# A hybrid retention, delta-net and RG-LRU block in fp32: mixer outputs, the delta net's values and keys and the retention's keys turned by VectorE in 32x32 blocks and stored with 128-byte runs

## The chip, the cores and the metric

The kernel runs on one core of a Trainium2 chip. The metric is the device time of one execution in microseconds, given as the median over several runs. One more execution was recorded by the hardware profiler; all views of the profile are from that one.

## The reference

Two layers work on one sequence of 1024 tokens with 1024 channels, all in float32. What matters here is the mixer of the first layer:

```
q_r,k_r,v_r,g_r, q_d,k_d,v_d,g_d, b_d,a_d = split(hn @ w_in)       # hn = rms_norm(h)
q_r, k_r = rotary(q_r), rotary(k_r)                                # 4 heads of 128
y_r = rms(retention_chunkwise(q_r, k_r, v_r)) * silu(g_r)          # chunks of 128
q_d,k_d,v_d = silu(causal_conv(...)); q_d,k_d = l2norm(q_d), l2norm(k_d)
y_d = rms_norm(gated_delta_chunkwise(q_d, k_d, v_d, g, beta), gain) * silu(g_d)
h = h + concat(y_r, y_d) @ w_out
```

In the delta net every chunk computes u = T (beta v - ... k S), out = (q S) + (masked q k^T) u, and S = S * decay + k_tail^T u, where T is the inverse of a triangular matrix. The retention has the same shape without the triangular solve. Before the mixers stands an RMS norm, behind each layer a convolutional feed-forward network; the second layer's mixer is a gated linear recurrence.

## The kernel before, in words

Activations lie with channels on the 128 partitions and tokens along the free axis. A float32 matrix is split into a high and a low part, and each product is three matmuls, lines 313, 314 and 315 (one "slot" in the code). A weight quarter of 128x512 is loaded by SyncE's queue (line 257), cast by ScalarE to its high part (line 267) and subtracted by VectorE (line 268); the rings hold six split quarters and seven raw ones. A projection of 128 output channels is 48 such matmuls: two halves of 512 tokens, 8 slots each. Each half has a PSUM bank of the tag "pp", of which there are four, and so has each output tile of the mixers.

The first mixer (`_mix0`) projects one unit of 128 channels after another. The order around the change is: the delta net's keys (kept in K), its queries, two gates, its values (`conv_head("v", h)`, convolution at lines 1263 to 1268), one more gate, and then, per head, the retention's query and key (`rot_head`: the rotary product is lines 1537, 1539 and 1540 on VectorE and line 1541 on GpSimd). The triangular inverses of the delta net are made from 32x32 blocks by `merge` (lines 1368 to 1399), one per head, with steps on TensorE and ScalarE in turn. They run beside the projections: a lane takes one step every two slots.

After the values, two lanes run beside the retention's projections:

- `scans` takes the delta net's eight chunks in order. `scan_inside` prepares a chunk: the decay mask (lines 1452, 1454), the values scaled by beta (line 1461), the scores k q (lines 1464, 1465), the scaled key tail (line 1473). `scan_state` does the chain: k S (line 1484), v minus it (line 1486), T v (line 1490, copied by ScalarE in line 1492 to u), k_tail^T u (line 1497), the new state (line 1502), and the output (lines 1507, 1508).
- `ret_half` takes one head and 512 tokens: scores (1576), key tail (1586), kv (1591), the states (1597, 1599), output (1605, 1606). It has one buffer for the values (`rvt`) and one for the key tail (`rkt`).

An output tile goes through `normalise`: square on ScalarE (1414), row sums and scaling on VectorE, a power on GpSimd (1421), the product (1423), and eight slots later `post`.

Five places turn 128x128 tiles by a TensorE matmul against the identity: `post` (line 1428, tokens to channels, copied out of PSUM by ScalarE in line 1429 and stored by ScalarE's queue), the delta net's values (line 1460) and keys (line 1472), and the retention's keys (line 1584).

The program's order on each engine is not the order of the code: a scheduler places the instructions by priority and by its own estimate of when they are ready, except in stretches marked as manual. Each engine then runs its list strictly in order, each instruction waiting for semaphores. At most eight DMAs of the SyncE and ScalarE queues use eight semaphores in turn.

Of the kernel before, what the change touches and what calls it, by code (L numbers as in the profile page):

```python
# [13 lines left out]
F32 = mybir.dt.float32  # L14
# [5 lines left out]
P = 128  # L20
# [3 lines left out]
HALF = 512  # L24
# [79 lines left out]
class Block:  # L104
# [1039 lines left out]
    def mix0(self, gain):  # L1144
        tc = self.tc
        self.q_dram = tc.dram_tile([NCH, P, HALF], F32, name="q_dram")
        self.v_dram = tc.dram_tile([NCH, P, HALF], F32, name="v_dram")
        self.gc_dram = tc.dram_tile([NH, NCH, P], F32, name="gc_dram")
        self.l_dram = tc.dram_tile([P, 32, 32], F32, name="l_dram")
        self.t_dram = tc.dram_tile([2, P, 32, 32], F32, name="t_dram")  # L1150
        self.y_dram = tc.dram_tile([8, P, T], F32, name="y_dram")
        self.rv_dram = tc.dram_tile([NCH, P, HALF], F32, name="rv_dram")
        self.g_dram = tc.dram_tile([NH, P, T], F32, name="g_dram")
        self.X = [[(self.slots1(4 * k + n), self.slots1(4 * k + 2 + n)) for n in range(2)] for k in range(KT)]
        with tc.tile_pool(name="l0", bufs=1) as pool:
            gd = self._mix0(pool.tile([P, 24 * HALF], F32, name="l0"))
        self.s2_stack = ExitStack()
        self.open_s2(self.s2_stack)
        self._mix0_out(gain, gd)
# [10 lines left out]
    def _mix0(self, room):  # L1170
# [239 lines left out]
        def normalise(o, eps, ydst, i):  # L1410
# [13 lines left out]

            def post():
                p = self.pc()
                for h in range(4):
                    PE.transpose(p[:, hs(h)], on[:, hs(h)], self.ident)
                A.copy(s, p)
                nc.scalar.dma_start(ydst, ps4(s) if len(ydst.shape) == 3 else s)  # L1430
# [11 lines left out]
        def scan_load(n):  # L1442
            t = chunk[n]
            t.update({"q": tmp2("qc"), "v": spare["v"][n % 2], "e": spare["e"][n % 2], "kt": spare["kt"][n % 2]})
            nc.sync.dma_start(t["v"], self.v_dram[n])
            nc.sync.dma_start(t["q"], self.q_dram[n])

        def scan_inside(n):
# [9 lines left out]
            pv = self.pc()  # L1458
            for h in range(NH):
                PE.transpose(pv[:, hs(h)], v[:, hs(h)], self.ident)  # L1460
            V.tensor_tensor(ps4(v), ps4(pv), bc_last(cn(cv), P), ALU.mult)
# [7 lines left out]
            if n < NCH - 1:  # L1469
                p = self.pc()  # L1470
                for h in range(NH):
                    PE.transpose(p[:, hs(h)], K[h][:, cs], self.ident)
                V.tensor_tensor(ps4(kt), ps4(p), bc_last(cn(ekt), P), ALU.mult)
            yield

        def scan_state(n):
# [32 lines left out]
            normalise(o, cn(irho), self.y_dram[4:8, :, cs].rearrange("h p c -> p h c"), 0)  # L1509
# [58 lines left out]
        def ret_half(h, i, q, k):  # L1568
# [4 lines left out]
            nc.sync.dma_start(ps4(vt), self.rv_dram[n0:n0 + 4, :, hs(h)].rearrange("n p c -> p n c"))  # L1573
            p = self.pc()
# [7 lines left out]
            p = self.pc()  # L1582
            for c in range(4):
                PE.transpose(p[:, hs(c)], k[:, cs(c)], self.ident)
            kt = tmp2("rkt")
            A.activation(kt, p, AF.Copy, scale=ktail[:, h:h + 1])
# [20 lines left out]
            normalise(o, None, self.y_dram[h][:, sl], 1)  # L1607
# [103 lines left out]

        def gates2(heads):
# [5 lines left out]
        for h in range(NH):  # L1718
            v = conv_head("v", h, None)
            nc.sync.dma_start(self.v_dram[:, :, hs(h)].rearrange("n p c -> p n c"),  # L1720
                              v.rearrange("p (n c) -> p n c", n=NCH))
# [19 lines left out]
        for h in range(NH):  # L1741
            q = rot_head(h)
            k = rot_head(4 + h)
            ret += [ret_half(h, i, q, k) for i in range(2)]
# [7 lines left out]
    def _mix0_out(self, gain, gd):  # L1752
# [10 lines left out]
        def gate(y):  # L1763
# [6 lines left out]
            nc.sync.dma_start(s, self.y_dram[y])  # L1770
# [93 lines left out]
```

## Time and profile before

| what | us |
|---|---|
| median of 3 runs | 2154.96 (2153.32 to 2155.97) |
| the profiled execution | 2152.99 |
| its span, first to last instruction | 2151.2 |
| TensorE busy (99%) | 2137.9 |
| VectorE busy (79%) | 1693.5 |
| ScalarE busy (50%) | 1082.8 |
| GpSimd busy (5%) | 98.2 |

Each line of a group in the profile names the source line, the engine, the operation, the tile it writes and those it reads, the shape, and how often; then busy time, the mean of one instruction in ns, and the idle time of the engine in front of it with what ended it. In the timeline a row has its start, its length, the engine and line. Tiles of the mixer's room are all called "l", those of the keys and the inverses "h". Matmuls overlap in the pipeline, so what a matmul costs is the distance between starts and not its length. The mean granted TensorE clock of the execution is 0.999.

### The profile page before, as it was taken

Reading aid. Unit: us, or ns where it says so; the run is one execution under the profiler, and the core shown is the slowest. Engines: PE = TensorE matmul, PEld = TensorE weight load, DVE = VectorE, ACT = ScalarE, POOL = GpSimd, SP = SyncE. Lnnn points to the kernel's source line nnn. Section 1 sums busy time; section 2 is a strip of 40 time slices with the busy share of each in tenths; the row PEclk is TensorE's granted clock in tenths of the full one; section 3 lists DMA queues with packets and bytes.
Section 4 is the critical chain, followed back from the end, with each engine's and each line's share of the span. In section 5 each row is a group of like instructions: output and inputs, shape, how many; then the busy total and the mean of one; then the engine's idle time right before and its main releaser. Section 6 shows DMA issues by size and latency. Waiting matters only on the chain.

```text
span 2151.2 us, 29709 instructions
## 1 busy us (share of the span) xinstructions
PE 2137.9 (99%) x10716; PEld 1783.3 (83%) x10716; DVE 1693.5 (79%) x2565; ACT 1082.8 (50%) x1748; POOL 98.2 (5%) x114
## 2 busy tenths in 40 slices
PE   9999999999999999999999999999999999999998
PEld 7877889888888888888888888888888888888887
DVE  7995676656999889888866787778999889888645
ACT  6444433235665555555324476756655555554321
POOL 0102022300000000000000000000000000000001
PEclk9999999999999999999999999999999999999999
DMA  5354423444145445437636312242354345375542
GB/s 187 92 168 127 134 89 96 166 128 131 55 155 174 146 158 191 156 109 273 230 104 205 87 54 80 70 154 68 119 180 167 143 159 178 118 266 178 181 169 84
DMA packets 205171, 307.98 MB, mean 143 GB/s; under 512 B 29376, under 2 KB 92384, under 8 KB 205024
## 3 DMA queue, kind: packets, MB, share of 16 engines
q1 hardware_dynamic: 197760, 299.60, 41.9%
q10 hardware_dynamic: 6240, 5.97, 0.9%
q8 instruction: 84, 1.38, 0.3%
q0 software_dynamic: 1024, 0.53, 0.1%
q14 instruction: 63, 0.52, 0.1%
HBM read 215.27 MB, written 90.74 MB: 142 GB/s over the span
## 4 chain that ended last, share of the span: by engine, by line
PE 93%; DVE 3%; DMA 1%; issue 1%; SPq 0%; ACT 0%; POOL 0%; POOLq 0%; DVEq 0%; ACTq 0%
PE ps L313 28%; PE ps L314 28%; PE ps L315 28%; PE pc L313 1%; PE pc L314 1%; PE pc L315 1%; DVE l L1333 0%; DVE l L1331 0%; PE pc L483 0%; DMA l<-gc_dram 0%; DVE wlo L268 0%; PE ps L1508 0%; PE pc L1464 0%; PE ps L1606 0%; PE pc L1576 0%
## 5 line engine op out<-in xcount | busy, mean ns | idle before, releaser
L313 PE MATMUL ps<-s,whi 128*128 128x512 f32 (+1 forms) x2704 | 1054.5, 391 | 1.1 <-ACT s L383 0.7
L314 PE MATMUL ps<-s,whi 128*128 128x512 f32 (+1 forms) x2704 | 1047.9, 388 | 0.5 <-DVE s L900 0.5
L315 PE MATMUL ps<-s,wlo 128*128 128x512 f32 (+1 forms) x2704 | 1047.3, 388 | 0.0
L267 ACT CAST whi<-raw 128x512 fp32r<-128x512 f32 (+1 forms) x620 | 376.6, 613 | 628.4 <-PE ps L314 494.6
L313 PEld LDWEIGHTS ps<-s,whi 128*128 128x128 f32 x2704 | 507.8, 188 | 106.6 <-ACT s L383 1.3
L315 PEld LDWEIGHTS ps<-s,wlo 128*128 128x128 f32 x2704 | 507.7, 188 | 104.7 <-DVE wlo L268 0.6
L314 PEld LDWEIGHTS ps<-s,whi 128*128 128x128 f32 x2704 | 508.1, 188 | 102.5 <-DVE s L900 1.9
L268 DVE TENSOR_TENSOR wlo<-raw,whi 128x512 fp32r<-128x512 f32 (+1 forms) x620 | 415.7, 676 | 72.0 <-ACT whi L267 60.8
L828 DVE SCALAR_TENSOR_TENSOR t<-halo,cols,t 128x1024 f32<-128x1024 f32 x176 | 221.6, 1281 | 2.6 <-ACT t L826 1.6
L801 DVE TENSOR_TENSOR halo<-ps,kept 128x512 f32<-128x512 f32 (+1 forms) x138 | 91.8, 666 | 74.4 <-PE ps L315 73.2
L811 DVE TENSOR_TENSOR h<-ps,h 128x512 f32<-128x512 f32 x112 | 77.3, 690 | 78.8 <-PE ps L315 78.8
L826 ACT ACTIVATE t<-halo,cols 128x1024 f32<-128x1024 f32 x88 | 109.5, 1246 | 18.6 <-DVE halo L801 10.2
L796 ACT COPY kept<-ps 128x512 f32<-128x512 f32 (+1 forms) x138 | 77.1, 558 | 11.0 <-PE ps L315 9.5
L533 DVE TENSOR_TENSOR h<-ps,h 128x512 f32<-128x512 f32 (+1 forms) x72 | 45.2, 630 | 42.4 <-PE ps L315 42.3
L916 DVE TENSOR_TENSOR t<-t 128x1024 f32<-128x1024 f32 x44 | 53.6, 1219 | 0.0
L911 ACT ACTIVATE t<-t 128x1024 f32<-128x1024 f32 x44 | 46.7, 1062 | 10.5 <-DVE t L828 10.5
L852 ACT CAST t<-t 128x512 fp32r<-128x512 f32 x56 | 34.0, 621 | 35.3 <-DVE t L916 33.2
L401 ACT ACTIVATE t<-h 128x512 f32<-128x512 f32 (+1 forms) x49 | 27.3, 562 | 43.6 <-DVE h L533 43.6
L313 PE MATMUL ps<-s,s 128*128 128x256 f32 (+1 forms) x144 | 46.0, 320 | 0.0
L314 PE MATMUL ps<-s,s 128*128 128x256 f32 (+1 forms) x144 | 45.8, 318 | 0.0
L315 PE MATMUL ps<-s,s 128*128 128x256 f32 (+1 forms) x144 | 45.8, 318 | 0.0
L857 DVE TENSOR_TENSOR t<-t 128x512 f32<-128x512 f32 x64 | 43.9, 685 | 0.7 <-DMA sf_dram<-t 0.6
(339 smaller groups left out, 2124.5 us busy)
## 6 DMA issues: line engine op xcount, KB each, us to landing
raw<-in_ffn_up_dram SPq DMA_DIRECT2D x176, 256.0 KB, 2.7
s<-pf_dram SPq DMA_DIRECT2D x112, 256.0 KB, 5.3
sf_dram<-t SPq DMA_DIRECT2D x72, 256.0 KB, 2.5
raw<-in_ffn_w_dram SPq DMA_DIRECT2D x64, 256.0 KB, 2.9
t<-sf_dram SPq DMA_DIRECT2D x58, 256.0 KB, 4.5
pf_dram<-t SPq DMA_DIRECT2D x56, 256.0 KB, 2.6
pf_dram<-lo SPq DMA_DIRECT2D x56, 256.0 KB, 2.5
raw<-in_mix_in_dram SPq DMA_DIRECT2D x52, 256.0 KB, 2.9
```

Source lines behind the costliest of these rows:

```text
L267: self.nc.scalar.copy(hi[:, 0:w], raw[:, 0:w])
L268: eng.tensor_tensor(lo[:, 0:w], raw[:, 0:w], f32(hi[:, 0:w]), ALU.subtract)
L313: mm(ps, whi, xhi, start=start, stop=False)
L314: mm(ps, whi, xlo, start=False, stop=False)
L315: mm(ps, wlo, xhi, start=False, stop=stop)
L796: A.copy(kept[o], ps)
L801: V.tensor_tensor(dst(i, j), v(ps), v(kept[k]), ALU.add)
L811: V.tensor_tensor(h(*to[o]), ps.rearrange("p (h c) -> p h c", c=256), h(*to[o]), ALU.add)
L826: A.activation(t, buf[:, 2:2 + T], AF.Identity, scale=w(0), bias=self.col(f"ffn_cb{layer}", tile_i))
L828: V.scalar_tensor_tensor(t, buf[:, 2 + j:2 + j + T], w(j), t, ALU.mult, ALU.add)
L911: A.activation(tg, tg, AF.Silu)
L916: V.tensor_tensor(tg, tg, tv, ALU.mult)
```

## The change

All five kinds of TensorE transposes go, and their PSUM tiles with them.

- `normalise` turns its product `on` with one VectorE 32x32 block transpose into `s`; `post`, still eight slots later, issues four stores from ScalarE's queue, one per 32 channels of the block, with runs of 128 bytes, which put the blocks in their places. The retention's outputs go to a new tensor `ry_dram` in blocks of 128x128.
- `store_turned` turns a whole head (128x1024) on VectorE into a tile of the three-deep pool "t" and stores it with four SyncE DMAs of 128 KB, 1024 runs of 128 bytes each. It is used for the delta net's keys and values behind each value head, and for the retention's keys behind each rotary key.
- The scans load the turned values and keys (the keys are a new load of 256 KB per chunk), and the scalings by line 1461 and 1473 read them in SBUF. `ret_half` loads its turned key into `rkt` and scales it there.
- The gates load `ry_dram` with 512-byte runs.

```diff
         self.ry_dram, self.k_dram, self.rk_dram: three new DRAM tensors
@@ normalise
+            V.transpose(s, on)
             def post():
-                p = self.pc()
-                for h in range(4):
-                    PE.transpose(p[:, hs(h)], on[:, hs(h)], self.ident)
-                A.copy(s, p)
-                nc.scalar.dma_start(ydst, ps4(s) if len(ydst.shape) == 3 else s)
+                for a in range(4):
+                    bs = slice(32 * a, 32 * a + 32)
+                    nc.scalar.dma_start(ydst[:, :, bs], s[bs].rearrange("j (b i) -> j b i", i=32))
@@ scan_load
+            if n < NCH - 1:
+                nc.sync.dma_start(t["kt"], self.k_dram[n])
@@ scan_inside
-            pv = self.pc()
-            for h in range(NH):
-                PE.transpose(pv[:, hs(h)], v[:, hs(h)], self.ident)
-            V.tensor_tensor(ps4(v), ps4(pv), bc_last(cn(cv), P), ALU.mult)
+            V.tensor_tensor(ps4(v), ps4(v), bc_last(cn(cv), P), ALU.mult)
...
-                p = self.pc()
-                for h in range(NH):
-                    PE.transpose(p[:, hs(h)], K[h][:, cs], self.ident)
-                V.tensor_tensor(ps4(kt), ps4(p), bc_last(cn(ekt), P), ALU.mult)
+                V.tensor_tensor(ps4(kt), ps4(kt), bc_last(cn(ekt), P), ALU.mult)
@@ ret_half
+            kt = tmp2("rkt")
+            nc.sync.dma_start(ps4(kt), self.rk_dram[n0:n0 + 4, :, hs(h)].rearrange("n p c -> p n c"))
...
-            p = self.pc()
-            for c in range(4):
-                PE.transpose(p[:, hs(c)], k[:, cs(c)], self.ident)
-            kt = tmp2("rkt")
-            A.activation(kt, p, AF.Copy, scale=ktail[:, h:h + 1])
+            yield
+            A.activation(kt, kt, AF.Copy, scale=ktail[:, h:h + 1])
@@ new
+        def store_turned(dram, x, h):
+            t = self.t()
+            V.transpose(t, x)
+            to = dram.rearrange("n (b i) c -> i (n b) c", i=32)
+            for d in range(4):
+                bs = slice(32 * d, 32 * d + 32)
+                nc.sync.dma_start(to[:, :, h * P + 32 * d:h * P + 32 * d + 32],
+                                  t[bs].rearrange("i (b j) -> i b j", j=32))
@@ value heads
-            nc.sync.dma_start(self.v_dram[:, :, hs(h)].rearrange("n p c -> p n c"),
-                              v.rearrange("p (n c) -> p n c", n=NCH))
+            store_turned(self.k_dram, K[h], h)
+            store_turned(self.v_dram, v, h)
@@ rotary keys
             k = rot_head(4 + h)
+            store_turned(self.rk_dram, k, h)
```

The lists of the engines change beyond the removed rows. Lines of the changed kernel are 3 higher than before in `merge`; line 1716 is the store of `store_turned`, line 1712 its transpose, line 1463 the scaling of the values (1461 before), line 1536 the first rotary product (1537 before). First SyncE's list behind the first values. Before; t_dram holds the 32x32 inverses that `merge` loads, and the two rows of t_dram here are those of the last merge, of head 3:

```order
L1720 DMA v_dram<-t 128x8x128
L1352 DMA l_117<-t_dram 32x4x32 x4
L257 DMA raw<-in_mix_in_dram 128x512 x2
L1352 DMA l_117<-t_dram 32x4x32 x4
L1720 DMA v_dram<-t 128x8x128
```

The same place now, from the store of head 2's values on:

```order
L1716 DMA v_dram<-t 32x32x32 x4
L1355 DMA l_120<-t_dram 32x4x32 x8
L1716 DMA k_dram<-t 32x32x32 x4
L1716 DMA v_dram<-t 32x32x32 x4
L1722 DMA g_dram<-t 128x1024
L257 DMA raw<-in_mix_in_dram 128x512
L1448 DMA kept<-v_dram 128x512
```

The last merge's loads stood behind the store of head 0 and now stand behind that of head 2. Then TensorE at that merge. Before; the rows of lines 313 to 315 are the projection beside it:

```order
L1368 MATMUL pc<-l_117,h_95 32x32 x16
L313 MATMUL ps<-s_96,whi 128x512
L314 MATMUL ps<-s_96,whi 128x512
L315 MATMUL ps<-s_96,wlo 128x512
L313 MATMUL ps<-s_96,whi 128x512
L314 MATMUL ps<-s_96,whi 128x512
L315 MATMUL ps<-s_96,wlo 128x512
```

Here 12 projection matmuls stand between every two steps of the merge, and 66 between its last step and the first scan. Now:

```order
L1380 MATMUL pc<-l_120 32x32 x7
L1384 MATMUL pc<-l_120 32x32 x8
L1394 MATMUL pc<-l_120,h_95 64x64 x8
L1400 MATMUL pc<-l_120 64x64 x4
L315 MATMUL ps<-s_96,wlo 128x512
L313 MATMUL ps<-s_96,whi 128x512
L1400 MATMUL pc<-l_120 64x64 x4
```

The last merge begins 138 projection matmuls behind the end of the merge before it (24 before), has 7 between its first and its last step (36 before), and 17 between its last step and the first scan (66 before). Last VectorE, from the end of that merge (L1399, now L1402) to the first scaling of values. Before:

```order
L1399 TENSOR_SCALAR h_95<-pc 64x4x64 x2
L1268 SCALAR_TENSOR_TENSOR t<-t 128x1024
L373 TENSOR_TENSOR t<-ps,R 128x512
L1737 TENSOR_TENSOR halo_99<-halo_99,R 128x1024
L268 TENSOR_TENSOR wlo<-raw,whi 128x512
L1452 TENSOR_TENSOR kept<-kept,l_117 128x512
L373 TENSOR_TENSOR t<-ps,R 128x512
L268 TENSOR_TENSOR wlo<-raw,whi 128x512
L1167 SCALAR_TENSOR_TENSOR t<-t 128x1024
```

Now, where L1170 is the gate's product and rows 1536 to 1539 are rotary products, nine of them between L1170 and L1457:

```order
L1402 TENSOR_SCALAR h_95<-pc 64x4x64 x2
L1170 SCALAR_TENSOR_TENSOR t<-t 128x1024
L1536 TENSOR_TENSOR t<-ps,halo_98 128x512
L1538 TENSOR_TENSOR l_120<-ps,halo_99 64x512
L1539 TENSOR_TENSOR l_120<-ps,halo_99 64x512
L1536 TENSOR_TENSOR t<-ps,halo_98 128x512
L1538 TENSOR_TENSOR l_120<-ps,halo_99 64x512
L1539 TENSOR_TENSOR l_120<-ps,halo_99 64x512
L1536 TENSOR_TENSOR t<-ps,halo_98 128x512
L1538 TENSOR_TENSOR l_120<-ps,halo_99 64x512
L1539 TENSOR_TENSOR l_120<-ps,halo_99 64x512
L1457 TENSOR_TENSOR kept<-kept,l_120 128x512
```

The three rotary halves stand in front of the first chunk's mask and values; before, one stood there. Behind L1457 follow a weight's subtraction (L268) and the values (L1463).

More of the change, by code (lines that the diff above doesn't have):

```diff
@@ L1146, in mix0 @@
         self.q_dram = tc.dram_tile([NCH, P, HALF], F32, name="q_dram")
+        self.ry_dram = tc.dram_tile([4, NCH, P, P], F32, name="ry_dram")
+        self.k_dram = tc.dram_tile([NCH, P, HALF], F32, name="k_dram")
+        self.rk_dram = tc.dram_tile([NCH, P, HALF], F32, name="rk_dram")
         self.v_dram = tc.dram_tile([NCH, P, HALF], F32, name="v_dram")
@@ L1508, in scan_state @@
                 PE.matmul(o[:, hs(h)], e[:, hs(h)], u[:, hs(h)], start=n == 0, stop=True)
-            normalise(o, cn(irho), self.y_dram[4:8, :, cs].rearrange("h p c -> p h c"), 0)
+            normalise(o, cn(irho), self.y_dram[4:8, :, cs].rearrange("h (d j) c -> j (h d) c", j=32), 0)
             yield
@@ L1606, in ret_half @@
                 PE.matmul(o[:, hs(c)], sc[:, hs(c)], vt[:, hs(c)], start=n == 0, stop=True)
-            normalise(o, None, self.y_dram[h][:, sl], 1)
+            normalise(o, None, self.ry_dram[h, n0:n0 + 4].rearrange("c (d j) x -> j (c d) x", j=32), 1)
         def together(*gens):
@@ L1769, in gate @@
             s = self.next_halo()[:, 4:4 + T]
-            nc.sync.dma_start(s, self.y_dram[y])
+            if y < 4:
+                nc.sync.dma_start(s.rearrange("p (n c) -> p n c", n=NCH), self.ry_dram[y].rearrange("n p c -> p n c"))
+            else:
+                nc.sync.dma_start(s, self.y_dram[y])
             V.scalar_tensor_tensor(g, g, 0.5 if y < 4 else self.og, s, ALU.mult, ALU.mult)
```

## The prediction, made before the change was run

> **What bounds the kernel now.** I read the page, then busy time by stage (the windows), then the groups by line and shape, then TensorE's timeline. The page's first line:
>
> ```profile
> PE 2137.9 (99%) x10716; PEld 1783.3 (83%) x10716; DVE 1693.5 (79%) x2565; ACT 1082.8 (50%) x1748; POOL 98.2 (5%) x114
> ```
>
> TensorE is busy 2137.9 of 2151.2 us. The stage that the change touches, from the values to the end of the scans:
>
> ```profile
> core 0: us, PE busy (x) PEld busy (x) DVE busy (x) ACT busy (x) POOL busy (x), PEclk, DMA share, GB/s
> 180.00:240.00 60.00, 59.74 (x658) 47.45 (x659) 31.50 (x38) 37.07 (x88) 12.08 (x22) 1.00 0.36 101
> 240.00:300.00 60.00, 60.00 (x364) 51.73 (x363) 41.88 (x68) 22.31 (x52) 10.23 (x8) 1.00 0.37 115
> 300.00:360.00 60.00, 60.00 (x413) 54.39 (x412) 43.39 (x90) 19.79 (x43) 18.37 (x15) 1.00 0.34 101
> ```
>
> TensorE has no idle time from 240 to 360 us, and VectorE is busy for some 70% of it. So TensorE work taken out is time won, as long as nothing makes TensorE wait; and a wait of TensorE costs its full length.
>
> **What is removed.** The transposes are these groups, 156 matmuls in 39 groups of four:
>
> ```profile
> L1428 PE MATMUL pc<-ident,l 128*128 128x128 f32 x64 | 9.6, 272 | 0.0
> L1584 PE MATMUL pc<-ident,t 128*128 128x128 f32 x32 | 4.8, 273 | 0.0
> L1472 PE MATMUL pc<-ident,h 128*128 128x128 f32 x28 | 4.2, 272 | 0.0
> L1460 PE MATMUL pc<-ident,l 128*128 128x128 f32 x16 | 2.4, 272 | 0.0
> L1460 PE MATMUL pc<-ident,kept 128*128 128x128 f32 x16 | 2.4, 272 | 0.0
> ```
>
> Their busy times (23.4 us) overlap with neighbours, so I price a group by starts, from TensorE's timeline:
>
> ```profile
> 282.79 0.39 PE L315 MATMUL ps<-s,wlo 128*128 128x512 f32 x1
> 283.02 0.60 PE L1428 MATMUL pc<-ident,l 128*128 128x128 f32 x4
> 283.38 0.47 PE L313 MATMUL ps<-s,whi 128*128 128x512 f32 x1
> 283.69 0.39 PE L314 MATMUL ps<-s,whi 128*128 128x512 f32 x1
> 283.91 0.39 PE L315 MATMUL ps<-s,wlo 128*128 128x512 f32 x1
> ```
>
> A projection matmul follows the last by 0.23 us (282.79 to 283.02). From L315 to the second matmul behind the group it is 0.90 us, of which two steps of 0.23 remain: a group costs 0.44, and 39 of them 17.0 us. ScalarE loses 16 copies too, which no path waits for.
>
> **What is added beside other work.** VectorE gets 16 transposes of 128x512 and 12 of 128x1024. The only one of that kind and size in the trace is
>
> ```profile
> L413 DVE STREAM_TRANSPOSE t<-t 128x512 f32<-128x512 f32 x2 | 1.4, 712 | 0.1
> ```
>
> that is 16 x 0.71 + 12 x 1.42 = 28 us, which fit into the 30% of some 200 us that VectorE has free; if they didn't, each would delay a PSUM tile's release by at most 1.4 us, and the projections have four banks of 5.5 us each. ScalarE issues 64 stores in place of 16, SyncE 48 stores for 4 and 15 more loads; the issue itself:
>
> ```profile
> L1430 ACTq DMA_DIRECT2D y_dram<-lo x8: 333/367/398, 284.3 to 437.5; - x8
> v_dram<-t SPq DMA_DIRECT2D x4, 512.0 KB, 4.1
> l<-rv_dram SPq DMA_DIRECT2D x8, 256.0 KB, 3.1
> kept<-v_dram SPq DMA_DIRECT2D x4, 256.0 KB, 3.0
> ```
>
> 0.37 us each, 48 x 0.37 = 18 us more on ScalarE less 16 copies of 0.59, over 200 us in which it is a third busy. I cost this at nothing. What matters is how long the stores take. The trace has 128-byte runs in the l_dram stores; in a window that holds little else:
>
> ```profile
> DMA packets 432, 0.05 MB, mean 21 GB/s; under 512 B 432, under 2 KB 432, under 8 KB 432
> q1 hardware_dynamic: 432, 0.05, 13.6%
> l_dram<-h SPq DMA_DIRECT2D x4, 16.0 KB, 1.5
> ```
>
> 13.6% of 16 engines over 2.3 us is 5.0 us for 432 packets: 11.6 ns each. A turned head is 4096 packets, 256 per engine: 3.0 us at that price. The other bound is the store of a head with 512-byte runs: 4.1 us to landing, less the 1.5 us that a small store takes, for 64 packets per engine is 41 ns each, 10.4 us for a head. I take 5 us, nearer the row with the same runs. The Trainium skill, "DMA: Bandwidth & Descriptors", section Specifications, says that writes below 512 bytes are done as read-modify-write and miss line rate; the 11.6 ns speak against a large penalty, but at a light load, so that is weighed as a rival below.
>
> **What is added on the path: waits that come with the new order.** The lists above are what each engine will do in order, so I follow TensorE through the places where producer and consumer have come close. Durations:
>
> ```profile
> 234.50 0.69 PE L1368 MATMUL pc<-l,h 32*32 32x32 f32 x32
> L1385 ACT ACTIVATE l<-pc 32x128 f32<-32x128 f32 x16 | 4.3, 270 | 0.3
> L1393 ACT COPY l<-pc 64x256 f32<-64x256 f32 x8 | 2.9, 366 | 3.7 <-PE pc L1391 3.6
> L1398 ACT COPY h<-l 128x512 f32<-128x512 f32 x8 | 5.0, 622 | 0.0
> L1399 DVE TENSOR_SCALAR h<-pc 64x256 f32<-64x256 f32 x8 | 3.2, 413 | 2.5 <-PE pc L1397 2.4
> L1166 ACT ACTIVATE t<-t 128x1024 f32<-128x1024 f32 x8 | 8.5, 1061 | 2.7 <-DVE t L373 2.7
> L1167 DVE SCALAR_TENSOR_TENSOR t<-t 128x1024 f32<-128x1024 f32 x8 | 9.8, 1226 | 4.3 <-ACT t L1166 4.3
> L1537 DVE TENSOR_TENSOR t<-ps,halo 128x512 f32<-128x512 f32 x16 | 11.0, 689 | 8.9 <-PE ps L315 8.5
> L1541 POOL TENSOR_TENSOR t<-t,l 128x512 f32<-128x512 f32 x16 | 24.0, 1501 | 113.2 <-DVE l L1540 74.7 <-DMA g_dram<-t 38.6
> L1456 ACT ACTIVATE l<-l 128x128 f32<-128x128 f32 x16 | 5.1, 388 | 0.0
> 284.84 1.05 PE L1490 MATMUL pc<-l,h 128*128 128x128 f32 x8
> 285.73 0.50 PE L1576 MATMUL pc<-t 128*128 128x128 f32 x3
> ```
>
> The last row pair gives 0.89 us per group of four fp32 matmuls.
>
> (a) The last merge. It started at 234.5; 114 more projection matmuls in front of it put it at 234.5 + 114 x 0.23 = 260.6. From its first matmul to its last it needs two copies (0.5), about eight 0.27 us pieces (2.2), then copies of 0.37 and 0.62 in turn (1.4), with TensorE steps of some 0.3 to 1.0 between: 6.0 us. TensorE has 4.5 us to do in it, so it idles 1.5.
>
> (b) The first values. Counted from the merge's start: VectorE ends L1402 at 6.6, the gate's tanh on ScalarE stands behind the merge's copies and ends at 6.8, its product at 8.1. Then three rotary halves of 3 x 0.69, where the second and third must also wait for GpSimd's 1.5 us on the one buffer: to 16.1. The mask, a weight's subtraction and the scaling of values, 0.7 each: 18.2. TensorE, after the merge, has 17 matmuls (3.9) and one group (0.9), and is at T v (L1490) at 10.8. It waits 7.5 us. Before, 66 matmuls covered this.
>
> (c) Its copy to u stands on ScalarE behind the decay exps of two chunks, pieces of 0.39 that follow each other by 0.32, the second chunk's behind VectorE's next mask (19.6): 22.8. TensorE reaches k_tail^T u at 20.1 and waits 2.7.
>
> (d) Later. At three places (heads 0, 2 and 3) `rvt` is reloaded only after the last output matmul of the half before, and the kv matmul (L1591) follows 2.7 us later, where issue and landing take 0.4 + 3.1 + 0.3: 1.1 us each, 3.3. For head 1 the turned key needs, from its transpose to L1591, store (0.4 for its issue, 5, 1.5), load (0.4 + 3.1) and scaling (0.7): 11.1 us, and TensorE's list has 9.6 there: 1.5 us. Heads 0 and 2 have over 12 us there, head 3 over 14.
>
> Sum: 17.0 removed, 1.5 + 7.5 + 2.7 + 3.3 + 1.5 = 16.5 added, -0.5 us. Against the profiled execution's own 2152.99 us that is 2152.5; the median of the runs is 2.0 above it, so I expect a median of 2154.5 us. What a measurement here can tell from no change is about 0.2%, 4.3 us.
>
> **Rivals.** 1. The waits hide. If VectorE and ScalarE reach (b) and (c) earlier than I count, say because the rotary halves need no GpSimd wait and the exps overlap, some 3 to 16 us of the 16.5 are not paid. For it: the whole before has no such wait, and (d) hangs on tenths. Against it: (b) is a chain of single instructions in one list. With half the waits paid it is 17.0 - 8.3 = 8.7 us faster, 2146; with none 2138.
>
> 2. The 128-byte stores are slow, slower kernel. Eight heads' stores queue behind each other; value head 2 went out at about 235 before and now goes out behind head 3's first rows on VectorE, near 245. Head 3's values then land at 245 + 4d + 1.5 with d the time of a head's store, and the load takes 3.4 more. It decides from d = 7 us on, 27 ns a packet: then the values arrive after 278, where (b) ends. At 10.4 us it is 13 us late, and in (d) head 1 waits 5 us more and head 2, with 1 to spare, 4: 22 us, 2176.5. For it: the 512-byte row's bound; against it: the l_dram row. By the read-modify-write rule of the same page of the Trainium skill d would be in that upper part.
>
> 3. The clock falls in the wait of (b). The kernel's first matmuls, after idling, against later ones of the same shape:
>
> ```profile
> L1624 PE MATMUL pc<-t 128*128 128x128 f32 x20 | 4.2, 396 | 1.2 <-POOL l L1627 1.2
> L1576 PE MATMUL pc<-t 128*128 128x128 f32 x64 | 8.4, 275 | 0.0
> ```
>
> The first 20 took 4.2 us at 0.21 each, later ones go at about 0.11 a pass: TensorE lost some 2 us there. A 7.5 us wait could bring that once or twice: 2 to 4 us more, 2156.5 to 2158.5. The Trainium skill, "TensorE: Matmul & The Clock Gate", Part 1, says that after an idle window of about 3.4 us the array runs at half clock until it was busy for such a window; the trace before has no idle gap of that length to show it.
>
> **How the numbers follow.** My forecast, waits that eat the gain, has 0.40; its own range, with d from 3 to 7 us and a third off or on the waits, is 2149 to 2160. The waits hide: 0.22. Slow stores: 0.20. The clock falls: 0.18, half of it beyond 0.2%. Faster is rival 1 and a little of the forecast, 0.24; slower is rival 2, half of rival 3 and some of the forecast, 0.36; within 0.2%: 0.40. The range leaves out the full gain and the slowest stores: 2145 to 2175.
>
> **What would show it.** Right: no L1428, L1460, L1472 or L1584 groups; TensorE idle of 10 to 13 us near 260 to 285, with T v waiting for VectorE's values and k_tail^T u for ScalarE's u; a few idle us at the kv matmul (now line 1589) for DMA; STREAM_TRANSPOSE 128x1024 near 1.4 us. Wrong: the stage without idle time (rival 1), or waits of VectorE for k_dram and v_dram stores that take over 8 us to land (rival 2), or a granted clock below 1 behind the gap (rival 3).

## The result, and the profile after

The changed kernel takes 2178.64 us (median of 4 runs, 2177.5 to 2179.39) against 2155.47 before (4 runs): 1.0112 times as long, 95% interval 1.0097 to 1.0126, 23.2 us slower. The profiled execution took 2179.39 us, its span is 2177.6 (2151.2 before), its mean granted clock 0.990 (0.999).

Busy time in windows of 60 us from the values on; the columns are those shown for the kernel before, with the clock as the third number from the end:

```profile
240.00:300.00 60.00, 49.49 (x313) 39.83 (x312) 35.80 (x46) 20.11 (x48) 6.63 (x5) 0.83 0.58 135
300.00:360.00 60.00, 57.66 (x359) 51.06 (x358) 44.65 (x89) 13.09 (x31) 14.56 (x11) 1.00 0.62 152
360.00:420.00 60.00, 47.99 (x282) 41.98 (x280) 40.45 (x83) 17.85 (x43) 14.37 (x11) 0.89 0.50 114
```

TensorE had no idle time here before; now it idles 10.5, 2.3 and 12.0 us, and in two of the windows the clock is below 1. What it waited for between 180 and 500 us (total, times, longest):

```profile
PE ps L313 <- DVE t L373: 4.2, 1, 4.2
PE ps L313 <- DVE l L1539: 4.1, 2, 2.5
PE ps L1506 <- DVE l L1426: 4.0, 1, 4.0
PE pc L1489 <- issue: 3.4, 1, 3.4
PE pc L1589 <- ACT l L1584: 2.9, 2, 2.5
PE pc L1466 <- DMA l<-q_dram: 2.5, 1, 2.5
PE pc L1489 <- DVE kept L1485: 1.7, 1, 1.7
PE pc L1483 <- DVE l L1501: 1.3, 1, 1.3
PE pc L1589 <- DMA l<-rv_dram: 0.9, 2, 0.7
...
PE pc L1489 <- DVE l L1485: 0.8, 1, 0.8
PE ps L1603 <- POOL l L1581: 0.8, 1, 0.8
...
```

With the two small rows left out (0.9 and 0.4) these are 27.9 us; before it was 0.7. Three places carry most of it.

**First place, the last merge.** TensorE's timeline:

```profile
260.51 0.39 PE L315 MATMUL ps<-s,wlo 128*128 128x512 f32 x1
260.83 0.24 PE L1371 MATMUL pc<-l,h 32*32 32x32 f32 x2
265.31 0.72 PE L313 MATMUL ps<-s,whi 128*128 128x512 f32 x1 [4.24 <-DVE t L373]
...
276.54 0.63 PE L315 MATMUL ps<-s,wlo 128*128 128x512 f32 x1
276.96 0.63 PE L313 MATMUL ps<-s,whi 128*128 128x512 f32 x1
```

It stops for 4.24 us, not in a step of the merge but for a PSUM bank that VectorE's line 373 has to empty. Behind it the projection matmuls follow each other by 0.42 us (276.54 to 276.96) in place of 0.23, up to 278.7: half the clock (the trace's record of the granted clock has a half from 265.4 to 279.0, 13.7 us). In these 13.4 us TensorE does the work of about 7, and loses some 6.3. VectorE at the same time:

```profile
259.68 1.23 DVE L1744 TENSOR_TENSOR halo<-halo,R 128x1024 f32<-128x1024 f32 x1 [3.79 <-DMA halo<-in_rope_dram]
260.82 1.22 DVE L1271 SCALAR_TENSOR_TENSOR t<-t 128x1024 f32<-128x1024 f32 x1
262.07 1.25 DVE L1712 STREAM_TRANSPOSE t<-h 128x1024 f32<-128x1024 f32 x1
263.24 1.20 DVE L1712 STREAM_TRANSPOSE t<-t 128x1024 f32<-128x1024 f32 x1
264.48 1.29 DVE L373 TENSOR_TENSOR t<-ps,R 128x512 f32<-128x512 f32 x2
```

Line 373 stands behind a wait of 3.79 us for the second rotary table and behind two turns, 2.4 us. The table's load is issued by ScalarE's queue, and late:

```profile
250.78 1.15 ACT L1266 ACTIVATE t<-halo,cols 128x1024 f32<-128x1024 f32 x1 [3.04 <-DVE t L1712]
255.98 0.33 ACTq L1742 DMA_DIRECT2D halo<-in_rope_dram  x1
```

The last value head's convolution, whose first step is L1266, waited 3.04 us for the turn of the head before it. It ended at 255.9 us (247.6 before), and the load was issued right behind it, at 256.0 in place of 247.7.

**Second place, the first scan.** SyncE's queue, then VectorE, then TensorE:

```profile
265.68 2.70 SPq L1716 DMA_DIRECT2D v_dram<-t  x4
277.70 0.34 SPq L1722 DMA_DIRECT2D g_dram<-t  x1
278.69 0.58 SPq L1448 DMA_DIRECT2D kept<-v_dram  x1
279.38 0.40 SPq L1449 DMA_DIRECT2D l<-q_dram  x1
```

```profile
284.77 0.69 DVE L1539 TENSOR_TENSOR l<-ps,halo 64x512 f32<-64x512 f32 x1
285.49 0.69 DVE L1457 TENSOR_TENSOR kept<-kept,l 128x512 f32<-128x512 f32 x1
287.78 0.68 DVE L1463 TENSOR_TENSOR kept<-kept,l 128x512 f32<-128x512 f32 x1
```

```profile
284.01 1.13 PE L1466 MATMUL pc<-l,h 128*128 128x128 f32 x8 [2.49 <-DMA l<-q_dram]
288.56 2.04 PE L1489 MATMUL pc<-kept,h 128*128 128x128 f32 x8 [3.42 <-issue]
292.67 1.16 PE L1496 MATMUL pc<-kept 128*128 128x128 f32 x8 [0.35 <-ACT kept L1491]
```

The values' store was issued by 268.4 and the loads of the scan only from 278.69 on, because the gate's store stands between them and waits for the gate's product. Then VectorE has the mask and the values (L1457, L1463) behind three rotary halves.

**Third place, the retention.** ScalarE's queue from 347 us on, then TensorE:

```profile
347.37 1.95 ACTq L1433 DMA_DIRECT2D y_dram<-lo  x4
356.24 3.69 ACTq L1433 DMA_DIRECT2D ry_dram<-l  x4
359.97 0.62 ACT L267 CAST whi<-raw 128x512 fp32r<-128x512 f32 x1 [17.08 <-DMA ry_dram<-l]
```

```profile
365.31 0.76 PE L1506 MATMUL ps<-l 128*128 128x128 f32 x2 [4.04 <-DVE l L1426]
368.55 0.80 PE L313 MATMUL ps<-s,whi 128*128 128x512 f32 x1 [2.47 <-DVE l L1539]
372.22 2.08 PE L1589 MATMUL pc<-l 128*128 128x128 f32 x8 [2.45 <-ACT l L1584]
375.80 0.63 PE L1603 MATMUL ps<-l 128*128 128x128 f32 x2
```

ScalarE stood 17 us with nothing but the eight small stores between two pieces of work, and TensorE then waited three times. The stores were not alone in it. The last four use semaphores of loads that SyncE had issued from 349.1 to 350.6 us, and each started as such a load had landed, 7.0 to 9.0 us after its issue; the last of these loads, of the values, landed at 359.6. VectorE waited for the same load:

```profile
359.62 0.69 DVE L1463 TENSOR_TENSOR l<-l 128x512 f32<-128x512 f32 x1 [3.42 <-DMA l<-v_dram]
```

From there VectorE's work follows without a gap up to the row sums of the next output tile (362.5 us), whose scaling (L1426) ended TensorE's first wait. So the late loads would have held that tile even with ScalarE free.

The eight passes of L1589 took 3.6 us with those of L1489 behind them (372.22 to 375.80), where two such groups took 2 x 0.89 before: half clock again, some 3.2 us lost up to 378, and some 1.7 behind the second place.

Together: 17.0 us of transposes gone, 27.2 us of waits come, and an estimated 11.2 us lost to the clock (6.3, 1.7 and 3.2), 21.4 of the 26.4 us by which the span grew. The other 5.0 I can't place in the trace.

### The profile page after: what moved, and what is told of

Read it like the earlier page. It is cut to its first block, busy times and chain, and to the rows that moved or that the text cites. A ratio compares the mean times of both kernels' runs of the same rounds, so it can differ in the third digit from the quotient of the medians.

```text
span 2177.6 us, 29523 instructions
## 1 busy us (share of the span) xinstructions
PE 2137.4 (98%) x10560; PEld 1777.6 (82%) x10560; DVE 1713.3 (79%) x2593; ACT 1073.6 (49%) x1732; POOL 98.5 (5%) x114
## 3 DMA queue, kind: packets, MB, share of 16 engines
q0 software_dynamic: 1024, 0.53, 0.1%
## 4 chain that ended last, share of the span: by engine, by line
PE 60%; issue 30%; DVE 4%; DMA 3%; POOL 1%; ACT 1%; SPq 0%; DVEq 0%; POOLq 0%; ACTq 0%
PE ps L313 18%; PE ps L314 18%; PE ps L315 18%; PE pc L313 1%; PE pc L314 1%; PE pc L315 1%; DMA l<-rk_dram 1%; PE ps L1555 0%; DMA l<-v_dram 0%; PE ps L1557 0%; PE ps L1556 0%; DVE h L973 0%; PE pc L1589 0%; DMA kept<-v_dram 0%; DMA kept<-k_dram 0%
## 5 line engine op out<-in xcount | busy, mean ns | idle before, releaser
L313 PE MATMUL ps<-s,whi 128*128 128x512 f32 (+1 forms) x2704 | 1053.7, 390 | 9.4 <-DVE t L373 4.2
L313 PEld LDWEIGHTS ps<-s,whi 128*128 128x128 f32 x2704 | 508.5, 188 | 116.2 <-issue 5.5
L268 DVE TENSOR_TENSOR wlo<-raw,whi 128x512 fp32r<-128x512 f32 (+1 forms) x620 | 417.4, 679 | 73.7 <-ACT whi L267 66.7
L313 PE MATMUL ps<-s,s 128*128 128x256 f32 (+1 forms) x144 | 46.0, 320 | 0.0
L373 DVE TENSOR_TENSOR halo<-ps,R 128x512 f32<-128x512 f32 x36 | 24.7, 688 | 25.7 <-PE ps L315 25.5
## 6 DMA issues: line engine op xcount, KB each, us to landing
raw<-in_ffn_up_dram SPq DMA_DIRECT2D x176, 256.0 KB, 2.7
s<-pf_dram SPq DMA_DIRECT2D x112, 256.0 KB, 5.2
sf_dram<-t SPq DMA_DIRECT2D x72, 256.0 KB, 2.5
raw<-in_ffn_w_dram SPq DMA_DIRECT2D x64, 256.0 KB, 2.9
t<-sf_dram SPq DMA_DIRECT2D x58, 256.0 KB, 4.8
pf_dram<-t SPq DMA_DIRECT2D x56, 256.0 KB, 2.6
pf_dram<-lo SPq DMA_DIRECT2D x56, 256.0 KB, 2.6
raw<-in_mix_in_dram SPq DMA_DIRECT2D x52, 256.0 KB, 3.6
```

The source lines that it names most:

```text
L268: eng.tensor_tensor(lo[:, 0:w], raw[:, 0:w], f32(hi[:, 0:w]), ALU.subtract)
L313: mm(ps, whi, xhi, start=start, stop=False)
```

## The experiments

The comparisons are with the kernel before, timed in the same rounds at 2153.6 to 2154.3 us.

### The three parts alone

In each, the other two parts of the change are put back as they were, with TensorE's transposes. For only_mixer_outputs these go from the change:

```diff
-            store_turned(self.k_dram, K[h], h)
-            store_turned(self.v_dram, v, h)
-            store_turned(self.rk_dram, k, h)
```

> Only the mixers' outputs are turned by VectorE and stored with 128-byte runs; values and keys are turned by TensorE as before. Theory A (TensorE waits where the new order brings producer and consumer together, and its clock falls behind such a wait): the order stays almost as before, 16 groups of 0.44 us go, so some 7 us less and at most 3 us of new waits: 2148 to 2152 us against 2155, granted clock 1.00 throughout. Rival B (the 64 small stores on ScalarE's queue hold ScalarE up, whatever the order): 4 to 8 us slower than before, with ScalarE idle in front of L267 for the stores. Rival C (the traffic of 128-byte runs makes the loads late): about the time before, 2154 to 2158.

Measured 2147.9 us, ratio 0.9974 (0.9965 to 0.9984): 5.9 us faster. ScalarE did sit idle for its small stores; TensorE did not wait for it. All that TensorE waited for from 150 to 520 us:

```profile
PE ps L313 <- ACT s L586: 1.8, 1, 1.8
PE pc L1371 <- DMA l<-t_dram: 1.3, 2, 1.0
PE ps L314 <- DVE s L587: 0.7, 1, 0.7
```

So 16 groups, priced at 7.0 us, brought 5.9, and rival B falls for this part. The profiled execution was the longest of the nine, 2152.42 us; in it the granted clock fell to a half twice, for 3.4 us each, behind waits that are all under 2 us.

In only_delta_net these go:

```diff
-            V.transpose(s, on)
-            store_turned(self.rk_dram, k, h)
```

> Only the delta net's values and keys are turned by VectorE. Theory A: the last merge lands where it is in the changed kernel; 15 groups go (6.6 us), and come: 4.2 us of waiting at the merge, some 6.7 us of half clock behind it, 6 us at the first values and 2 us of half clock there: 12 us slower, about 2167, with the granted clock near 0.83 from 240 to 300 us and 1.00 from 360 to 420. Rival B: ScalarE's queue has no such stores here, so 6 us faster, 2149. Rival C: the loads of values and keys are late throughout the scans, 5 to 10 us slower, but spread over 280 to 400 us and with the clock at 1.00 wherever no wait of over 3 us stands.

Measured 2170.55 us, ratio 1.0076 (1.0062 to 1.009): 16.7 us slower, more than theory A said, with the waits of the changed kernel at the first two places (4.5, 3.3 and 2.6 us) and a clock of 0.66 from 260 to 280 us.

In only_retention_keys these go:

```diff
-            V.transpose(s, on)
-            store_turned(self.k_dram, K[h], h)
-            store_turned(self.v_dram, v, h)
```

> Only the retention's keys are turned by VectorE. Theory A: the last merge stands as before; 8 groups go (3.5 us); the kv steps are crowded behind the key's round trip through DRAM, as in the changed kernel, where waits of 4.0, 2.5 and 2.5 us and 3.5 us of lost clock were seen from 360 to 380 us: 6 to 10 us slower, 2161 to 2165, with a clock under 1.00 only behind such waits. Rival B: no small stores on ScalarE's queue, so ScalarE isn't held and the waits at 360 don't come: 2152 to 2155. Rival C: small, 2152 to 2157.

Measured 2160.92 us, ratio 1.0032 (1.0019 to 1.0044): 7.1 us slower, about as theory A had it, though its longest wait is 3.0 us and not 4.0. The three parts sum to 17.9 us; the whole change costs 23.2, so some 5 us come only where they meet.

### Is it the place of the merge?

```diff
-                    (nc.sync if q else nc.gpsimd).dma_start(
+                    nc.gpsimd.dma_start(
```

> The whole change, with the half of the merges' loads that SyncE issued moved to GpSimd's queue. The last merge then stands in TensorE's list where it stood before the change (projection matmul 654 in place of 768), and the retention's order stays that of the changed kernel. Theory A: the 4.2 us wait, the 6.7 us of half clock behind it and part of the 6 us at the first values go: 11 to 16 us faster than the changed kernel, 2163 to 2168, with the clock at 1.00 around the merge. Rivals B and C (stores or traffic, not the order): within 3 us of the changed kernel, 2176 to 2180.

Measured 2178.99 us, ratio 1.0116 (1.0102 to 1.013): no gain; theory A as I had put it falls. TensorE's waits from 170 to 285 us:

```profile
PE pc L1371 <- DMA l<-t_dram: 3.9, 2, 3.2
PE ps L313 <- DVE t L373: 3.1, 1, 3.1
```

The merge stood in its old place, and the wait for L373 was still there: it belongs to VectorE's list and not to the merge. The first row is a new wait, of the first merge for its own loads, and took back what the rest may have gained.

### Tiles of their own

In `retention_own_tile` the turned key leaves pool "t":

```diff
-        self.wraw_p = pool("wraw", 7)
+        self.wraw_p = pool("wraw", 6)
-            store_turned(self.rk_dram, k, h)
+            for i in range(2):
+                t = self.tp.tile([P, HALF], F32, tag="turned", name="turned", bufs=1)
+                V.transpose(t, k[:, i * HALF:(i + 1) * HALF])
...
```

> Only the retention's keys are turned, as in only_retention_keys (2160.9 us), but in a tile of 128x512 of its own, half a head at a time; for its room the ring of raw weight quarters has six in place of seven. The same 128-byte runs are stored. Theory D: the next head's query no longer waits for a pool tile held by the half before, the kv steps are no longer crowded, and the wait of 3.0 us goes: 2149 to 2154 us. Rival C (the key's round trip and the stores cost by themselves): 2158 to 2162. If the smaller ring costs something, it shows outside 180 to 500 us, in the feed-forward part.

Measured 2151.48 us, ratio 0.9988 (0.9979 to 0.9997): 9.4 us better than only_retention_keys, and 2.2 faster than before. From 180 to 500 us TensorE waited once for over 0.6 us:

```profile
PE pc L1593 <- ACT l L1588: 1.6, 1, 1.6
```

The same bytes went out in the same runs, so rival C falls for this part. The edit is one of tile, half and ring together, and I did not separate them; the mechanism that fits is that pool "t" has three tiles and query, key and turned key take them all, so that the next query waits for the half before it.

In `delta_net_own_tiles` the delta net's turned copies go to free slots of the room, and the keys are turned behind each query:

```diff
             q = conv_head("q", h, None)
+            store_turned(self.k_dram, K[h], h)
...
             v = conv_head("v", h, None)
-            store_turned(self.k_dram, K[h], h)
-            store_turned(self.v_dram, v, h)
+            store_turned(self.v_dram, v, h, slots(18, 2))
```

> Only the delta net's values and keys are turned, as in only_delta_net (2170.6 us), but the turned copies are made in tiles of their own in the mixer's room instead of the three-deep pool "t", and the keys are turned and stored behind each query instead of behind each value head. The merges then stand in TensorE's list where they stood before the change. Theory D (a turned copy takes one of three pool tiles, so convolutions, the second rope load and the PSUM evacuations behind it on VectorE come late): the waits of 4.5, 3.3 and 2.6 us and the low clock behind them go, and what is left is the gain of 15 groups at 0.44 us, 6.6: 2147 to 2150 us, clock 1.00. Rival C (the 128-byte stores themselves, their traffic and their eight semaphores, make the loads late): still slower than before, 2158 or more, since the same bytes are stored.

Measured 2177.83 us, ratio 1.0113 (1.0099 to 1.0127). A miss, and partly one of my own making: the keys' turns fell into the triangular substitution, where VectorE is nearly full.

```profile
140.00:160.00 20.00, 10.57 (x44) 7.26 (x43) 15.13 (x35) 5.44 (x7) 0.00 (x0) 0.80 0.74 189
160.00:180.00 20.00, 15.42 (x60) 11.35 (x59) 18.27 (x51) 5.70 (x10) 0.00 (x0) 0.84 0.57 158
```

TensorE idled 14.0 us there. The wait for L373 was gone, but T v still waited 4.7 us. `all_own_tiles` (the whole change with both mends) and `outputs_and_delta_net` (without the retention's part) carry the same early keys.

> The whole change with both mends: keys and values of the delta net turned in tiles of their own, keys early, and the retention's keys in a tile of their own (six raw quarters). All 39 groups of TensorE transposes are gone. Theory D: 17.0 us gained less 3 to 5 us of waits that are left: 2140 to 2144 us. Rival C: about the time of the changed kernel, over 2165. Rival B (ScalarE held by its own small stores in the retention): in between, 2150 to 2160, with ScalarE idle in front of its work for the ry_dram stores as at 343 to 360 us in the changed kernel.

> As all_own_tiles, but the retention's keys are turned by TensorE as before, and the ring keeps seven raw quarters: mixer outputs and the delta net's keys and values turned by VectorE, in tiles of their own. 31 groups go, 13.6 us. Theory D: 2141 to 2145 us. Rival C: over 2160. Rival B: 2150 to 2156.

Measured 2180.83 us (ratio 1.0126, 1.0112 to 1.014) and 2174.2 us (1.0094, 1.008 to 1.0108); neither tells the theories apart, for that reason.

### Scans later, and all mends

```diff
-        gdn += [scans()]
             q = rot_head(h)
+            if h == 0:
+                gdn += [scans()]
```

> only_delta_net (2170.6 us) with one edit: the scans' lane is started behind the first rotary head in place of before it, so that TensorE has some 48 projection matmuls more (10.9 us) between the last value head and the first scan. Theory L (TensorE comes to the first values too early, since VectorE's list has their mask and scaling behind the gate's product and three rotary halves): the waits of 3.3 and 2.6 us in front of the first chunk and the 2 us of low clock behind them go, while the wait of 4.5 us for L373 and the half clock behind it, which come before the scans, stay: 2161 to 2164 us. Rival C (stores and loads are slow by themselves and only move along): 2168 to 2172.

Measured 2169.06 us, ratio 1.0069 (1.0057 to 1.0081): 1.5 us better. The waits at the first chunk shrank to 2.2 us, and others came in the retention (2.5 for an output tile, 2.3 for values): theory L is right about that wait and wrong about what its removal is worth.

The three mends are this one, the room's slots for both turned copies, and the merges' loads by head:

```diff
-            store_turned(self.k_dram, K[h], h)
-            store_turned(self.v_dram, v, h)
+            store_turned(self.k_dram, K[h], h, slots(16, 2))
+            store_turned(self.v_dram, v, h, slots(18, 2))
-                    (nc.sync if q else nc.gpsimd).dma_start(
+                    (nc.sync if q and h < 2 else nc.gpsimd).dma_start(
```

> Only the delta net's values and keys turned, with three mends: scans started one rotary head later, turned copies in tiles of their own in the room (each key still turned behind its value head), and the loads of the merges of heads 2 and 3 all on GpSimd's queue, so that they don't stand behind the stores on SyncE's. The merges stand in TensorE's list where they stood before the change. The same 128-byte runs are stored. Theories D and L (lists and tiles, not bytes): no wait of over 1 us between 180 and 320 us, clock 1.00, and the gain of 15 groups, 6.6 us: 2147 to 2151. Rival C: 2158 or more. If only the wait for L373 stays, 2156 to 2159.

Measured 2165.89 us, ratio 1.0062 (1.005 to 1.0074). TensorE's list was nearly that of before, and still 12 us were lost against before. The trace places most of them: from 150 to 520 us TensorE waits 12.7 us in all (1.3 before), the most for loads of `rv_dram` (4.2 us, the longest 2.5), and twice its clock is at a half for 3.4 us.

outputs_and_retention is only_mixer_outputs with the retention's edit of retention_own_tile.

> Mixer outputs and the retention's keys turned by VectorE, the keys in a tile of their own (six raw quarters); values and keys of the delta net turned by TensorE as before. If the parts add up: 5.9 less from only_mixer_outputs and 2.2 less from retention_own_tile, 2144 to 2147 us. Rival B (ScalarE's queue of small stores waits for semaphores that the retention's stores and loads hold): 2149 to 2156, with ScalarE idle for ry_dram stores and TensorE waiting for VectorE between 340 and 480 us.

Measured 2149.77 us, ratio 0.998 (0.9971 to 0.9988): faster than before, but less than the sum of its two parts. On top of the outputs the retention's part brings nothing more.

all_mends is the change with the edits of delta_net_three_mends and retention_own_tile.

> The whole change with all mends: scans later, own tiles for all turned copies (six raw quarters), merge loads of heads 2 and 3 on GpSimd's queue. All 39 groups are gone, 17.0 us. Theories D and L: 2139 to 2144 us. Rival B: 2146 to 2155, the waits in the retention. Rival C: over 2160.

Measured 2166.87 us, ratio 1.0062 (1.005 to 1.0074): 11.8 us better than the change (10.1 when each is compared with the kernel before in its own rounds), and above what theories D and L gave.

### Is it the runs of 128 bytes?

```diff
-            to = dram.rearrange("n (b i) c -> i (n b) c", i=32)
+            to = dram[:, :, hs(h)].rearrange("n p c -> p n c")
             for d in range(4):
-                nc.sync.dma_start(to[:, :, ...], t[bs].rearrange("i (b j) -> i b j", j=32))
+                nc.sync.dma_start(to[bs], t[bs].rearrange("p (n c) -> p n c", n=NCH))
```

> only_delta_net (2170.6 us) with the four stores of each turned head written in runs of 512 bytes in place of 128: same bytes, same four DMAs, same turns on VectorE and the same loads, so the blocks land in the wrong places and the output is not the reference's. TensorE's list is then that of before, but for the transposes. Theory O (the loss comes with the order, or with the 128-byte runs on the chip): the gain of 15 groups shows, 2146 to 2150 us. Rival N (the number of stores, the turns on VectorE or the new loads of keys): 2158 or more.

Measured 2153.34 us, ratio 0.9992 (0.9983 to 1.0001): 17.2 us better than only_delta_net by this one edit. The same view as above, from 150 to 520 us, without four rows of 0.3 to 0.6 us (the profiled execution was the shortest of its runs, 2150.2 us):

```profile
PE ps L1604 <- DVE l L1598: 1.9, 1, 1.9
```

The two turns and the product with the second rotary table stand in front of line 373 here too, from 249.6 to 255.2 us, and TensorE doesn't wait. The table's load was issued at 247.3, as before the change, and not at 256.0. In delta_net_three_mends, with short runs, the load is issued at 248.2 us, and the wait for line 373 is absent too. So the turns alone don't make the wait of the first place; in these runs it comes with the late load in front of them.

For one store the loop over d goes:

```diff
-            for d in range(4):
-                nc.sync.dma_start(to[bs], t[bs].rearrange("p (n c) -> p n c", n=NCH))
+            nc.sync.dma_start(to, t.rearrange("p (n c) -> p n c", n=NCH))
```

> As delta_net_long_runs, but with one store of 512 KB per turned head in place of four (blocks in the wrong places, as there). If the number of DMAs costs by the eight semaphores that they use in turn, this is faster than delta_net_long_runs by 2 us or more; if not, within 2 us of it: 2146 to 2150.

Measured 2150.42 us, ratio 0.9981 (0.9972 to 0.999): 2.9 us better than with four stores in the median, though the two intervals overlap and SyncE's list changes with the edit.

In the next two the long runs are put into delta_net_three_mends and into the changed kernel.

> delta_net_three_mends (2165.9 us) with stores in runs of 512 bytes (blocks in the wrong places). Its TensorE list differs in 16 of 9930 places. Theory S (the 128-byte runs are slow on the chip, whatever the order): 2147 to 2152, some 15 us faster. Theory M (the mends themselves cost: scans later, merge loads on GpSimd's queue): within 4 us of it, 2162 to 2168.

Measured 2156.77 us, ratio 1.0011 (1.0002 to 1.002): 9.1 us better than with short runs. Both theories have a share: the mends cost some 3 us by themselves (against delta_net_long_runs), and the runs, with what they change in the lists, 9. The waits for `rv_dram` are gone.

> The whole change with the stores of store_turned in runs of 512 bytes (keys and values in the wrong places), the outputs' stores as in the change, with 128 bytes. The last merge and the first scan stand where they stood before; the retention's kv steps are a little crowded. Theory O: 17.0 us gained less the 3 to 6 us of waits that the retention's keys and the outputs cost: 2141 to 2146 us. Rival N: 2160 or more.

Measured 2155.32 us, ratio 1.0005 (0.9996 to 1.0014): the whole loss of the change goes with the run length of these stores and the lists that follow from it, though the 17 us of gain don't appear. TensorE waits 5.4 us at one T v there.

### The runs or the lists?

The run length changes two things: what the chip has to do, and what the scheduler takes the stores to cost, and so every list. The last pair takes the second away.

```diff
         scan_row(0)
+        with tc.manual_schedule(engines={PE, DVE, Activation, SP}):
             gates2((0, 1))
...
```

The stretch reaches to the end of the mixer.

> only_delta_net (2170.6 us) with one edit: from the first gate behind the queries to the end of the mixer, the lists of TensorE, VectorE, ScalarE and SyncE follow the order of the code, as the stretches marked manual do, and not the scheduler's estimate. The stores are those with 128-byte runs, four for each head, in pool "t" as in the change. The merges, the first scan and the kv steps then stand in TensorE's list where they stood before the change. Theory O (the lists cost the 17 us that long runs won back): 2147 to 2154 us, with no wait of TensorE over 2.5 us and the clock at 1.00. Theory S (the runs themselves are slow on the chip): 2162 to 2172, with VectorE waiting for loads of v_dram or SyncE's queue standing behind stores.

Measured 2240.08 us, ratio 1.0398 (1.0384 to 1.0413). A miss: the order of the code is bad for other reasons (the merges wait up to 15.7 us for loads and ScalarE). But with these lists, the same row for row, the stores can be exchanged.

> delta_net_code_order (2240.1 us) with the stores of each turned head in runs of 512 bytes in place of 128 (blocks in the wrong places, so the output is not the reference's). All lists are the same, row for row. Theory O (the runs cost by the lists that the scheduler makes of them): the same time within 3 us, 2237 to 2243. Theory S (the runs themselves are slow on the chip, 17 us in the delta net's part): 2222 to 2228.

Measured 2234.63 us, ratio 1.037 (1.0356 to 1.0384): 5.5 us better, between the theories. How long the values' 16 stores and 8 loads took from issue to landing, first with 128 and then with 512 bytes:

```profile
DMA to landing us min/median/max: 2.6/3.1/6.4
```

```profile
DMA to landing us min/median/max: 2.1/2.3/6.3
```

So the runs themselves cost some 5 us with these lists held still, 0.8 us a transfer in the median. With the lists free they cost 17.2. That the other 12 are the lists' is a difference between two regimes and not a measurement; it fits the restored TensorE list in delta_net_long_runs, and three_mends_long_runs (9.1 us) fits it less well, since there SyncE's and VectorE's lists differ too.

## Why the prediction was wrong

It said 2154.5 us, and the kernel took 2178.64, outside the range.

**The gain of 17.0 us** was about right in kind: 16 groups priced at 7.0 us brought 5.9.

**"I cost this at nothing"** is the step that failed. The added work of VectorE, ScalarE and SyncE was compared with their free time on the average. The durations were right (128x512 measured 0.70 us, 128x1024 1.23 to 1.24), and the 28 us fitted; but two turns and a late load stood in one list in front of a PSUM evacuation (first place), and eight stores stood in ScalarE's list in front of its work, behind loads that landed late (third place). The claim that a turn delays a PSUM tile by at most 1.4 us left out that turns come in pairs, together with whatever they wait behind.

In the sum this shows as terms that it doesn't have. At its places (a) to (d) TensorE waited 14.3 us (4.24 + 5.9 + 0.35 + 3.8) against 16.5 forecast; that these are near each other is luck, since (a) was too low and the other three too high. Another 13.6 us of waits stand where the sum has nothing, and the 11.2 us of lost clock are not in it either.

**(a)** The merge started at 260.8, as worked out (260.6). Its idle time was 4.24 us in place of 1.5, for L373 and not for its own copies; merge_loads_on_gpsimd shows that the wait stays when the merge is moved.

**(b)** held in kind: the values stand behind three rotary halves, and TensorE waits 2.49 + 3.42 = 5.9 us (7.5 forecast), part of it for the queries, whose load the gate's store held up.

**(c)** was 0.35 us and not 2.7.

**(d)** came to 3.8 us at the kv matmul (L1589) against 4.8, with the shares the other way round: 0.9 for the reloaded values (3.3 forecast) and 2.9 for the key (1.5). What the sum had no term for are the other waits from 300 us on, 12.7 us: 4.1 for the PSUM banks of the retention's projections (L313 behind L1539), 4.0 for the delta net's output tile, 2.5 at T v, 1.3 at k S, 0.8 at the retention's output. I had followed the round trip of the key and not the tile that it holds; a tile of its own brought 9.4 us in retention_own_tile.

**Rival 3, the clock,** came at three places and cost some 11 us in place of 2 to 4. I had put it beside the forecast as another case, though its cause, a long wait, was part of the forecast. The Trainium skill, "TensorE: Matmul & The Clock Gate", Part 1, has half rate after an idle window of about 3.4 us and full rate after a window of sustained work. The first half agrees with the 4.24 us here, but in only_mixer_outputs half clock also came behind waits of 1.84 and 0.65 us, close together, so here no such window without work was needed. The way back took 13.7 us with the merge's small matmuls in it; in merge_loads_on_gpsimd, behind the wait of 3.13 us for L373, where projection matmuls alone follow, it took 3.4. That small matmuls keep the clock down fits both, and was not tested by itself.

**Rival 2, slow stores,** ended on the right side by another mechanism; that its 2176.5 us is near the measured time is luck. SyncE's last stores, in a window of 5.7 us:

```profile
DMA packets 7109, 0.91 MB, mean 160 GB/s; under 512 B 7108, under 2 KB 7108, under 8 KB 7108
q1 hardware_dynamic: 7108, 0.90, 113.8%
```

113.8% of 16 engines over 5.7 us for 7108 packets is 14.6 ns each, 3.7 us a head, under the 7 us from which that rival decides, and TensorE's wait at T v was for VectorE's list: the values landed at 283.2 us and were scaled from 287.78. The Trainium skill, "DMA: Bandwidth & Descriptors", section Specifications, speaks of read-modify-write for such writes; the 5.5 us of the last pair is what such runs cost here with the lists of the code's order held still.

What stays open: how the delta net's 17.2 us divide between the runs and the lists, beyond the 5.5 and 9.1 us measured with other lists, and why loads took 7.0 to 9.0 us at the third place.

The best version found is only_mixer_outputs, 2147.9 us, 0.9974 (0.9965 to 0.9984) of before. No version that also turned the delta net's values and keys, with the data in its right place, beat the kernel before.

## What to carry to other kernels

An engine that is 70% busy is not free for a microsecond at a given place: ask what stands directly behind the added work in that engine's list, and who waits for that. A buffer from a shared pool is part of a step's price, as is every queue that its stores go to, with the semaphores that it shares with loads. Where waits of several microseconds are forecast for TensorE, add the half clock behind each to the same forecast, and not as another case.

## What the runs showed of the hardware that I had not expected

A wait of 4.24 us was followed by 13.7 us at half the clock, more than the wait itself cost. In all traces here a stretch at half clock inside the mixer lasts a multiple of 3.41 us, from 3.4 to 20.5 us (delta_net_code_order), and it also came behind waits under 2 us (only_mixer_outputs). Transfers in runs of 128 bytes took 14.6 ns a packet under load (11.6 in the light load of the kernel before). The version with one DMA in place of four for the same 512 KB, with the same runs of 512 bytes, was 2.9 us faster over eight heads; how much of that is the DMAs themselves was not separated.
